# A three-layer network on one core: the delta rule's triangular inverses from blocks of 16 in place of 32, and a list scheduler that knows the array's tilings

## The chip, the cores and the metric

The kernel runs on one core of a Trainium2 chip. The core has a matrix engine (TensorE, PE in the profile, with its weight loads as PEld), VectorE (DVE), ScalarE (ACT), GpSimd (POOL) and a queue (SyncE, SP) from which DMAs are issued. The metric is device time in microseconds (us) per execution; lower is better.

## What is computed

A network of width 1024 on 512 tokens of x and 256 of context, batch 1. Block 1 has a gated delta rule mixer with 8 heads (GDN), a mixture of 16 experts on both regions, an SSD mixer with 8 groups, and a second mixture on x alone. Block 2 has an S5 and a short convolution mixer, a sparse attention (nsa), their projection (mix) and a feed-forward layer (ffn). The part that the change rewrites is the delta rule's solve. In the reference, per chunk and direction:

```python
kb = kc * bc[..., None]
lower = jnp.where(strict, jnp.einsum('nbhid,nbhjd->nbhij', kb, kc) * decay, 0.0)
rhs = jnp.concatenate([vc * bc[..., None], kb * jnp.exp(gcum)[..., None]], axis=-1)
sol = lax.linalg.triangular_solve(eye + lower, rhs, left_side=True, lower=True, unit_diagonal=True)
u, w = sol[..., :dv], sol[..., dv:]
attn = jnp.where(tril, jnp.einsum('nbhid,nbhjd->nbhij', qc, kc) * decay, 0.0)
def step(S, inp):
    q_i, k_i, u_i, w_i, a_i, g_i = inp
    v_new = u_i - jnp.einsum('bhck,bhkv->bhcv', w_i, S)
    o = (jnp.einsum('bhck,bhkv->bhcv', q_i * jnp.exp(g_i)[..., None], S)
         + jnp.einsum('bhij,bhjv->bhiv', a_i, v_new))
```

The kernel uses chunks of 128 tokens (6 of them: 4 of x, 2 of context) and inverts the unit triangular matrix of each chunk and direction explicitly.

## The kernel before, in words

**Recording and order.** All of a stage's code runs against a recorder (class Rec, line 53). Each instruction becomes an operation with the operations that it depends on and a cost in ns (cost, line 190); matmuls written under nc.together() are one operation. flush (line 243) turns the list into an order: schedule (line 307) is a list scheduler with simulated engines, which picks among up to 48 candidates per engine the one of highest priority that can start early enough. The priority is the place in the program less beta times the length of the work behind the operation, and an operation of lower priority goes first only if it can start more than tol ns sooner. flush takes the shortest of the (beta, tol) pairs that its caller gives, and emits the instructions in that order at line 304. So every instruction has line 304 in the profile, and each engine works through its own queue strictly in the emitted order. Costs in the model before: a matmul by its columns and passes, at one matmul at a time; a DMA lands 2.025 us after its issue at the earliest (1125 and 900 ns), and counts 2000 ns in the priorities. The callers' pairs: one for the GDN (line 946), one to four elsewhere.

**The GDN (line 577).** Each head projects q, k, v and z (px: matmuls with 512 and 256 columns over the two regions), forms G (k with k) and Hq (k with q), and from them L, the strictly triangular matrices of both directions in the two halves of one tile, and at. The inverse has two levels:

- Blocks of 32 on the diagonal. There are 4 x 6 x 2 = 48 per head. They go through DRAM (gdn_blocks, bscr in the code) into D32, one block per partition. DVE scales and masks them (two operations of 48 x 1024), and GpSimd inverts them row by row: 30 steps of two tensor_tensor each (x, then D). A memset sets the diagonal, ScalarE makes the transposed copy, one DMA takes both to DRAM (gdn_inverses, tscr in the code), and four DMAs bring them back as Td and Ud with chunks side by side. Eight ScalarE copies put Ud into U, whose off-diagonal blocks are zero.
- Joins to 64 and 128 on PE, for m = 32 and 64. pB multiplies L with the inverses at hand, ScalarE copies it to B, pU multiplies with the transposed inverses Tr, and ScalarE copies the negative into U. For m = 32 the transposed inverses are Td, for m = 64 PE makes them (pT).

The scan then runs 6 steps in each of the two directions: act_k with the state S, rt and U, vd with kT (the new state), vn with at, act_q with S. Behind it the outputs o are normalised on ACT and DVE, transposed on PE (oT), and go to DRAM. After all heads the out projection (op) follows; its last 48 matmuls belong to head 7. Some heads also carry rounds of the modulation (ada).

**The other stages** are recorded and ordered in the same way. In the SSD (line 1447) px and pcx are the projections, wl the low part of a weight tile that DVE makes for them, W the decay weights of a head: a DMA brings rows from DRAM (ssd_rows), ACT and DVE apply them, and py multiplies them with the inputs. In the mixtures eg, eu, ec and ey are the experts' matmuls, their weights come in pieces of 1 MB (we), and hT, pb, po, xs and others are transposes, gates, gather and scatter.

Of the kernel before, what the change touches and what calls it, by code (L numbers as in the profile page):

```python
# [52 lines left out]
class Rec:  # L53
# [4 lines left out]
    def __init__(self, nc, tc):  # L58
# [7 lines left out]
        self.slot_times = {}  # L66
        self.seen = set()
# [77 lines left out]
    def record(self, i, engine, method, a, k):  # L145
# [34 lines left out]
        cost = self.cost(engine, method, reads, writes, a, k)  # L180
        if i < len(self.ops):
# [4 lines left out]
            o["more"].append((method, a, k))  # L186
            return
        self.ops.append(dict(e=engine, m=method, a=a, k=k, preds=preds, names=names, cost=cost, psum=any(self.tiles.get(r[0], (0, 0, 0))[2] for r in rr + ww)))

    def cost(self, engine, method, reads, writes, a, k):  # L190
# [29 lines left out]
        if engine == "scalar":  # L220
            return (45.0 if psum else 95.0) + n / 1.2 + 93.0 * scalars + (90.0 if k.get("accum_out") is not None else 0)
# [21 lines left out]
    def flush(self, trials=((0.0, 30.0),)):  # L243
# [40 lines left out]
        cost = [2000.0 + o["cost"] / 360.0 if "dma" in o["m"] else o["cost"] for o in ops]  # L284
# [13 lines left out]
        self.span, self.seq, self.free_at, self.dma_free, times = best  # L298
# [8 lines left out]
    def schedule(self, static, beta, tol):  # L307
# [13 lines left out]
        for t, lst in order.items():  # L321
            for nm in lst:
                if nm in self.seen:
                    got.add(nm)
                    slots[t].remove(max(slots[t]))
                    alloc[t].add(pos[nm])
                    nxt[t] = pos[nm] + 1
        npred = [len(o["preds"]) for o in ops]
# [17 lines left out]
        while len(seq) < n:  # L346
            best = None
            for e, c in cand.items():
                fe = free_at[e]
                eb = None  # L350
                for r in c[: self.WINDOW]:
                    i = by[r]
                    st = max(fe, ready[i])
                    if eb is not None and st >= eb[0] - tol:
# [15 lines left out]
            if best is None:  # L370
                return math.inf, seq, free_at, dma_free, slots
# [15 lines left out]
            if "dma" in o["m"]:  # L387
                free_at[e] = st + 475.0
                dma_free = max(st + 1125.0, dma_free) + o["cost"] / 360.0
                fin = dma_free + 900.0  # L390
            else:
                fin = st + o["cost"]
                free_at[e] = fin
            end[i] = fin
# [12 lines left out]
        return max(end), seq, free_at, dma_free, slots  # L407
# [169 lines left out]
def gdn(K, H, apply, w, ba_w, conv_w, a_log, dt_b, norm_g, scr, bscr, tscr, rscr, side, xc, w_out, gate, route):  # L577
# [9 lines left out]
    es = ExitStack()  # L587
    K.ring(es, 15)
# [8 lines left out]
    low = per.tile([48, 32, 32], BF, name="low")  # L597
    for i in range(0, 32, 16):
        x = K.nm.tile([48, 16, 32], F32, name="low_f", tag="nm", bufs=3)
        m = K.cst[i:i + 16, 3, 0:32]  # L600
        nc.sync.dma_start(x, bass.AP(tensor=m.tensor, offset=m.offset, ap=[[0, 48]] + [list(z) for z in m.ap]))
        v.tensor_copy(low[:, i:i + 16, :], x)
# [86 lines left out]
    for h in range(NH):  # L689
# [75 lines left out]
        L = live.tile([128, 6, 128], F32, name="L", bufs=2)  # L765
        at = live.tile([128, 2, 6, 128], F32, name="at", bufs=2)
        for t0, t1 in ((0, 4), (4, 6)):
# [21 lines left out]
            for z in range(-1, 3):  # L789
                bl, cl, d = (slice(0, 128), slice(0, 128), 0) if z < 0 else (slice(32 * z, 32 * z + 32), slice(32 * z + 32, 128), 1)  # L790
                v.tensor_tensor(L[bl, t0:t1, cl], pT[bl, 0:n, cl], c_brk[d][bl, t0:t1, None].to_broadcast([bl.stop - bl.start, n, cl.stop - cl.start]), op=OP.mult)

# [3 lines left out]
        D32 = tmp.tile([48, 2080], F32, name="D32")  # L796
        nc.sync.dma_start(D32[:, 0:1056], bscr[h])
        T = D32[:, 0:1024].rearrange("p (i j) -> p i j", j=32)
        v.tensor_tensor(T, T, D32[:, None, 1024:1056].to_broadcast([48, 32, 32]), op=OP.mult)
# [6 lines left out]
        g_.memset(D32[:, 0:1024:33], 1.0)  # L806
# [1714 lines left out]
```

## Time and profile before

| | us |
|---|---|
| median of 3 timed runs | 3677.41 |
| the three runs | 3683.21, 3677.41, 3665.22 |
| the profiled execution | 3660.83 |
| its span | 3659.1 |

| engine | busy us | share of the span |
|---|---|---|
| PE | 3359.7 | 92% |
| PEld | 2255.5 | 62% |
| DVE | 1848.2 | 51% |
| ACT | 1181.0 | 32% |
| POOL | 555.4 | 15% |

The mean granted TensorE clock is 0.971 of the full 2.4 GHz. Since all instructions have one line, groups are told apart by tiles: px<-H,wl is the operation that writes px from H and wl. The stages by time: GDN to 774 us (its last sums and the routing to 870), first mixture to 1480, SSD to about 2014 and its out projection to 2160, second mixture to 2715, block 2 from there, with the attention in 2817 to 3013 and the feed-forward layer from 3289 to the end.

### The profile page before, as it was taken

To read this page: it belongs to the slowest core of one execution; us is meant where nothing else is said; L and a number is where in the kernel's file an instruction comes from. 1 tells how busy PE (TensorE), PEld (TensorE's weight loads), DVE (VectorE), ACT (ScalarE), POOL (GpSimd) and SP (SyncE) were. 2 spreads that over 40 slices of the span, in tenths; PEclk is the share of its full clock that TensorE was granted. 3 is DMA by queue.
4 is the path that set the end of the run, shared out by engine and by line. 5 is a ranking of instruction groups with operands and counts; after the bars stand their busy time and mean duration, and the time that the engine had idled before them with its cause. 6 is when DMAs were issued, how large, how long until landed. Compare 5 with 4: busy or idle time off the path is not lost. (4 is left out here: it accounts for less than half of the span.)

```text
span 3659.1 us, 55424 instructions
## 1 busy us (share of the span) xinstructions
PE 3359.7 (92%) x21505; PEld 2255.5 (62%) x21505; DVE 1848.2 (51%) x4086; ACT 1181.0 (32%) x2518; POOL 555.4 (15%) x753
## 2 busy tenths in 40 slices
PE   7987979899999999899999879888879999999999
PEld 4776765666344444677877654332257658878887
DVE  4666755562223222778778542452164564445542
ACT  3354543423111111355555321120032353333331
POOL 0646544301000000013222010010011000000000
PEclk9999989899999999999999889999999999999999
DMA  5522227455888888354241359999962303333322
GB/s 188 160 60 56 74 65 230 155 188 197 342 312 311 335 317 315 111 147 133 93 141 53 140 220 401 362 368 421 420 143 81 119 1 98 96 100 92 96 87 87
DMA packets 251652, 669.21 MB, mean 183 GB/s; under 512 B 72156, under 2 KB 85612, under 8 KB 202236
## 3 DMA queue, kind: packets, MB, share of 16 engines
q1 hardware_dynamic: 251388, 665.66, 51.4%
q8 instruction: 169, 2.77, 0.3%
q14 instruction: 95, 0.78, 0.1%
HBM read 644.26 MB, written 21.30 MB: 182 GB/s over the span
## 5 line engine op out<-in xcount | busy, mean ns | idle before, releaser
L304 DVE TENSOR_TENSOR wl<-w,wh 128x512 fp32r<-128x512 f32 (+3 forms) x452 | 323.1, 717 | 458.8 <-PE fu L304 68.0
L304 ACT ACTIVATE wh<-w 128x512 fp32r<-128x512 f32 (+3 forms) x500 | 307.7, 622 | 675.2 <-PE fu L304 120.7
L304 PE MATMUL eg<-we,xs 128*32 128x512 f32 (+1 forms) x1536 | 371.5, 596 | 8.3 <-DMA we<-moe_w 7.2
L304 PE MATMUL eu<-we,xs 128*32 128x512 f32 (+1 forms) x1536 | 322.3, 595 | 7.4 <-DMA we<-moe_w 7.4
L304 PE MATMUL ey<-we,hTs 128*32 128x512 f32 (+1 forms) x1536 | 295.1, 601 | 17.2 <-ACT hTs L304 9.0
L304 PE MATMUL px<-H,wl 128*128 128x512 f32 (+1 forms) x768 | 269.3, 372 | 21.4 <-DVE wl L304 21.3
L304 PE MATMUL px<-H1l,wh 128*128 128x512 f32 (+1 forms) x768 | 267.3, 364 | 0.0
L304 PE MATMUL px<-H,wh 128*128 128x512 f32 (+1 forms) x768 | 266.1, 370 | 0.5 <-ACT wh L304 0.3
L304 PE MATMUL ec<-we,xs 128*32 128x512 f32 x1024 | 235.2, 594 | 0.0
L304 DVE TENSOR_TENSOR yl<-ey,yh 64x512 fp32r<-64x512 f32 x64 | 44.1, 689 | 337.8 <-ACT yh L304 337.3
L304 PEld LDWEIGHTS eg<-we,xs 128*32 128x32 f32 (+1 forms) x1536 | 96.3, 118 | 140.2 <-issue 103.9
L304 POOL TENSOR_TENSOR wl<-w,wh 128x512 fp32r<-128x512 f32 x48 | 64.6, 1346 | 761.7 <-DVE H1l L304 658.1
L304 DVE SCALAR_TENSOR_TENSOR eth<-eth,eg 128x512 f32<-128x512 f32 x32 | 22.0, 687 | 310.8 <-ACT eth L304 310.8
L304 PEld LDWEIGHTS eu<-we,xs 128*32 128x32 f32 (+1 forms) x1536 | 91.9, 119 | 141.1 <-issue 105.8
L304 PEld LDWEIGHTS ey<-we,hTs 128*32 128x32 f32 (+1 forms) x1536 | 97.3, 120 | 127.6 <-issue 61.8
L304 PEld LDWEIGHTS px<-H,wl 128*128 128x128 f32 x768 | 143.1, 192 | 43.8 <-DVE wl L304 26.2
L304 ACT ACTIVATE eth<-eg 128x512 f32<-128x512 f32 x32 | 19.1, 595 | 462.0 <-PE eg L304 404.7
L304 PEld LDWEIGHTS px<-H,wh 128*128 128x128 f32 x768 | 144.3, 192 | 25.0 <-issue 6.1
L304 PEld LDWEIGHTS px<-H1l,wh 128*128 128x128 f32 x768 | 142.9, 192 | 18.6 <-issue 1.3
L304 PE MATMUL eyc<-we,hcTs 128*32 128x256 f32 x1024 | 140.9, 379 | 0.0
L304 POOL TENSOR_TENSOR D<-D,x 48x30 f32<-48x30 f32 (+14 forms) x240 | 133.7, 557 | 18.3
L304 POOL TENSOR_TENSOR x<-D 48x30 f32<-48x30 f32 (+14 forms) x240 | 127.0, 529 | 59.4 <-DVE D L304 41.5
(1040 smaller groups left out, 7564.1 us busy)
## 6 DMA issues: line engine op xcount, KB each, us to landing
we<-moe_w SPq DMA_DIRECT2D x384, 1024.0 KB, 7.9
w<-ada_w SPq DMA_DIRECT2D x192, 256.0 KB, 5.2
w<-w_gu SPq DMA_DIRECT2D x88, 256.0 KB, 3.4
w<-gdn_w SPq DMA_DIRECT2D x64, 256.0 KB, 3.1
w<-ssd_w SPq DMA_DIRECT2D x64, 256.0 KB, 3.1
w<-w_mix SPq DMA_DIRECT2D x48, 256.0 KB, 2.7
w<-w_dn SPq DMA_DIRECT2D x40, 256.0 KB, 2.6
w<-ssd_wz SPq DMA_DIRECT2D x32, 256.0 KB, 2.6
```

What stands on the lines that cost most here:

```text
L304: getattr(getattr(self.nc, o["e"]), m)(*a, **k)
```

## The change

Two parts. **The inverse.** The diagonal blocks have 16 rows and there are 96 of them, one per partition, in Dz, which also holds the transposed copies. GpSimd's chain has 14 steps instead of 30. They go out in two DMAs and come back as Td and Ud in the old form, with pairs of 16-blocks on the diagonal of 32-blocks. The join from 16 to 32 is new: qB multiplies L (for one direction) and Lb (for the other, a new tile of DVE) with Ud, DVE masks it with half into B16, qU multiplies with Td, and DVE writes Ud less qU into U (four operations, in place of ScalarE's eight copies). The join m = 32 now makes its transposes with pT, as m = 64 did.

**The order.** array gives each matmul a tiling of the array (its rows and columns rounded to 32, 64 or 128), a place in it and a time. schedule lets matmuls at different places overlap, and a change of tiling waits for the array to drain and 94 ns more. DVE operations that touch SBUF alone wait while GpSimd works. A DMA lands 500 ns later and counts 2500 ns, some strided ScalarE reads cost twice, and PE's times are divided by a clock of the stage (0.94 GDN, 0.99 mixtures, 0.96 SSD). Every flush tries 15 pairs of beta and tol and keeps the shortest. Instructions outside the GDN are the same in another order.

```diff
@@ class Rec @@
+    SWITCH = 94.0
...
+    def port(self, engine, method, reads, writes):
...
+        return engine == "gpsimd" or engine == "vector" and not any(self.tiles.get(x.tensor.name, (0, 0, 0))[2] for x in reads + writes)
...
+    def array(method, a):
...
+        size = lambda x: 32 if x <= 32 else 64 if x <= 64 else 128
+        lhs, n = a[1], free(a[2])
+        rows, cols = size(lhs.ap[0][1]), size(free(lhs))
+        r0, c0 = (x.offset // x.ap[0][0] % 128 if x.ap[0][0] else 0 for x in (lhs, a[0]))
...
+        d = (2 if two else 1) * n / 2.4 + (13.5 if lhs.dtype == F32R else 4.0)
...
+        return (rows, cols), (r0 // rows, c0 // cols), (2 if two else 1) * d
@@ cost @@
+            n *= 2 if any(x.ap[-1][0] > 16 and n > 512 for x in reads if x.ap[-1][1] > 1) else 1
@@ flush @@
-    def flush(self, trials=((0.0, 30.0),)):
+    TRIALS = tuple((b, t) for b in (0.0, 0.2, 0.4, 0.6, 1.0) for t in (0.0, 30.0, 90.0))
...
+    def flush(self, trials=TRIALS):
...
-        cost = [2000.0 + o["cost"] / 360.0 if "dma" in o["m"] else o["cost"] for o in ops]
+        cost = [2500.0 + o["cost"] / 360.0 if "dma" in o["m"] else o["cost"] for o in ops]
@@ schedule @@
+                    if e == "tensor":
+                        tiling, place, _ = ops[i]["pe"][0]
+                        st = max(st, held.get(place, 0.0) if tiling == mode else drained + self.SWITCH)
+                    elif e == "vector" and ops[i]["port"]:
+                        st = max(st, port)
...
-                fin = dma_free + 900.0
+                fin = dma_free + 1400.0
+            elif e == "tensor":
+                fin = at = st
+                for tiling, place, t in o["pe"]:
+                    t /= clock
+                    if tiling != mode:
+                        if mode is not None:
+                            at = max(at, drained + self.SWITCH)
+                        mode, held = tiling, {}
...
@@ gdn @@
-        for j in range(1, 31):
-            sh = [48, 31 - j, j]
-            x = tmp.tile([48, 240], F32, name="x32", bufs=2)[:, 0:sh[1] * sh[2]].rearrange("p (i j) -> p i j", j=j)
-            g_.tensor_tensor(x, T[:, j + 1:32, j:j + 1].to_broadcast(sh), T[:, j:j + 1, 0:j].to_broadcast(sh), op=OP.mult)
-            g_.tensor_tensor(T[:, j + 1:32, 0:j], T[:, j + 1:32, 0:j], x, op=OP.add)
+        for j in range(1, 15):
+            sh = [96, 15 - j, j]
+            x = tmp.tile([96, 64], F32, name="x16", bufs=2)[:, 0:sh[1] * sh[2]].rearrange("p (i j) -> p i j", j=j)
+            g_.tensor_tensor(x, T[:, j + 1:16, j:j + 1].to_broadcast(sh), T[:, j:j + 1, 0:j].to_broadcast(sh), op=OP.mult)
+            g_.tensor_tensor(T[:, j + 1:16, 0:j], T[:, j + 1:16, 0:j], x, op=OP.add)
...
-        for z in range(4):
-            bl = slice(32 * z, 32 * z + 32)
-            for d in range(2):
-                s.activation(U[bl, d, :, bl], Ud[bl, 1 - d], AF.Copy)
+        p = K.ps([128, 2, 6, 32], "qB")
+        with nc.together():
...
+                        pe.matmul(p[bl, d, t, :], Lb[bl, t, :] if d else L[bl, t, bl], Ud[bl, d, t, :], start=True, stop=True, skip_group_check=True)
+        B = tmp.tile([128, 2, 6, 32], F32, name="B16")
+        v.tensor_tensor(B, p, half[:, :, None, :].to_broadcast([128, 2, 6, 32]), op=OP.mult)
+        p = K.ps([128, 2, 6, 32], "qU")
+        with nc.together():
...
+                        pe.matmul(p[bl, d, t, :], Td[bl, d, t, :], B[bl, d, t, :], start=True, stop=True, skip_group_check=True)
+        for bl in rows:
+            v.scalar_tensor_tensor(U[bl, :, :, bl], p[bl], -1.0, Ud[bl], op0=OP.mult, op1=OP.add)
...
-    nc.flush(GDN_TRIALS)
+    nc.flush()
...
-GDN_TRIALS = ((0.4, 0.0),)
```

**The order, place 1: PE, the join of a head.** x24 is a group of 24 matmuls; p with a number is a matmul of the scan. Before, head 1 (an odd head):

```order
L304 MATMUL pB<-Ud,L 32x32 x24
L304 MATMUL row<-cst,cols 6x128
L304 MATMUL G<-act_k 128x128 x3
L304 MATMUL pU<-B_753,Td 32x32 x24
L304 MATMUL G<-act_k 128x128 x3
L304 MATMUL Hq<-act_q,act_k 128x128 x3
L304 MATMUL pT<-cst,U_337 64x64 x12
L304 MATMUL pB<-U_337,L 64x64 x12
L304 MATMUL GT<-cst,GE 128x128 x6
L304 MATMUL Hq<-act_q,act_k 128x128
L304 MATMUL pU<-B_758,Tr 64x64 x12
L304 MATMUL px<-H_313,wl 128x512
```

Head 2 (an even head) has only its own pB, pU, pB, pT, pU in one run, and then the scan. After, head 1:

```order
L340 MATMUL px<-H_319,wl 128x256
L340 MATMUL qU<-B_729,Td 32x32 x48
L340 MATMUL row<-cst,cols 6x128
L340 MATMUL pT<-cst,U_337 32x32 x24
L340 MATMUL pB<-U_337,L 32x32 x24
L340 MATMUL pU<-B_734,Tr_732 32x32 x24
L340 MATMUL pB<-U_337,L 64x64 x12
L340 MATMUL pT<-cst,U_337 64x64 x12
L340 MATMUL pU<-B_739,Tr_737 64x64 x12
L340 MATMUL p_743<-vb,U_337 128x128
L340 MATMUL p_750<-vb,U_337 128x128
L340 MATMUL p_748<-vn,at 128x128
```

The next head's G and Hq, which stood between the steps of the join, now stand ahead of qU; the px matmuls that stood within the scan stand behind it and ahead of qB. The same run of join and scan is found in heads 0 to 4, with four ada matmuls in head 4's join. The scan's matmuls stand in pairs, one of each direction.

**Place 2: PE, the end of the GDN, where head 7's outputs are transposed (oT).** Before:

```order
L304 MATMUL op<-H1l,wh 128x512
L304 MATMUL oT<-cst,o 128x128 x2
L304 MATMUL op<-G_2397,wl 128x512
L304 MATMUL oT<-cst,o 128x128 x3
L304 MATMUL op<-G_2398,wh 128x512
L304 MATMUL oT<-cst,o 128x128
L304 MATMUL op<-H1l,wh 128x512
```

After:

```order
L340 MATMUL p_2212<-rt,U_337 128x128
L340 MATMUL p_2219<-rt,U_337 128x128
L340 MATMUL p_2214<-vn,at 128x128
L340 MATMUL p_2221<-vn,at 128x128
L340 MATMUL oT<-cst,o 128x128 x6
L340 MATMUL op<-H1l,wh 128x512 x4
```

Before, oT stood among the out projection's matmuls with 158 of them behind it; after, it stands right behind head 7's scan with the last 48 behind it. The others moved ahead of the scan, into head 7's join.

**Place 3: DVE in the SSD, one head.** fm and y are the head's activations. Before, where these five rows come in each of four heads, and in a fifth with one wl:

```order
L304 SCALAR_TENSOR_TENSOR y<-y,sz_15111 128x512
L304 SCALAR_TENSOR_TENSOR fm_15182<-pcx,cw,fm_15182 128x255
L304 SCALAR_TENSOR_TENSOR W<-R,cs,W 128x128 x2
L304 TENSOR_TENSOR wl<-w,wh 128x512 x2
L304 SCALAR_TENSOR_TENSOR fm_15182<-th,fm_15182 128x768
```

After:

```order
L340 SCALAR_TENSOR_TENSOR fm_16233<-th,fm_16233 128x768
L340 SCALAR_TENSOR_TENSOR W<-R,cs,W 128x128 x8
L340 SCALAR_TENSOR_TENSOR y<-y,sz_16154 128x512
L340 TENSOR_TENSOR wl<-w,wh 128x512
L340 SCALAR_TENSOR_TENSOR y<-y,sz_16162 128x512
```

Two operations on W stood right ahead of wl; now eight stand together, with an operation on y between them and wl, and other heads have other neighbours.

## Rows read from the trace of the kernel before

**Rows 1.** Table of windows: window, its length, busy us of each engine, PEclk, DMA share, GB/s.
```profile
47.00:774.00 727.00, 638.95 (x4962) 506.09 (x4964) 450.34 (x1216) 317.78 (x761) 329.68 (x559) 0.94 0.38 115
...
870.00:1480.00 610.00, 599.95 (x5435) 267.39 (x5427) 163.08 (x345) 85.65 (x173) 0.29 (x2) 1.00 0.82 319
...
1520.00:2014.00 494.00, 464.61 (x2649) 390.51 (x2647) 394.73 (x788) 264.29 (x581) 129.19 (x90) 0.98 0.35 110
...
2160.00:2715.00 555.00, 485.43 (x2398) 203.04 (x2397) 205.02 (x457) 101.75 (x185) 40.14 (x29) 0.98 0.93 362
...
2817.00:3013.00 196.00, 184.36 (x891) 115.73 (x891) 124.37 (x391) 84.97 (x236) 0.00 (x0) 0.97 0.17 57
```

**Rows 2.** PE's waits in 47:774: in total, times, longest.
```profile
PE pB L304 <- DMA Ud<-gdn_inverses: 13.0, 5, 9.9
PE pB L304 <- DVE D L304: 12.9, 1, 12.9
PE pU L304 <- ACT B L304: 8.8, 5, 3.3
...
PE pB L304 <- POOL D L304: 2.7, 1, 2.7
PE pB L304 <- ACT U L304: 2.2, 2, 1.1
```

**Rows 3.** Timeline: start, length. GpSimd's last steps (head 0); head 4's way to pB.
```profile
173.61 0.23 POOL L304 TENSOR_TENSOR x<-D 48x30 f32<-48x30 f32 x1
173.92 0.24 POOL L304 TENSOR_TENSOR D<-D,x 48x30 f32<-48x30 f32 x1
...
474.24 0.15 POOL L304 MEMSET D<- 48x32 f32 x1
...
483.92 1.22 DVE L304 TENSOR_TENSOR D<-D 48x1024 f32<-48x1024 f32 x1 [5.19 <-DMA D<-gdn_blocks]
...
485.19 0.86 PE L304 MATMUL pB<-Ud,L 32*32 32x32 f32 x48 [12.85 <-DVE D L304]
```

**Rows 4.** Timeline of PE, early in the GDN.
```profile
53.70 0.40 PE L304 MATMUL baT<-H,wl 128*32 128x512 f32 x1
53.94 0.39 PE L304 MATMUL px<-H1l,wh 128*128 128x512 f32 x1
54.16 0.40 PE L304 MATMUL px<-H,wl 128*128 128x512 f32 x1
...
73.80 0.39 PE L304 MATMUL px<-H1l,wh 128*128 128x512 f32 x1
74.12 0.43 PE L304 MATMUL ba<-cst,ba__380 32*128 32x32 f32 x4
```

**Rows 5.** Timeline of PE, head 0's first join group at full clock.
```profile
186.94 0.61 PE L304 MATMUL pB<-Ud,L 32*32 32x32 f32 x48 [0.49 <-DMA Ud<-gdn_inverses]
```

**Rows 6.** Table of windows, the bare joins of heads 0 and 4.
```profile
187.00:199.50 12.50, 5.37 (x169) 4.72 (x169) 7.12 (x11) 9.02 (x23) 7.21 (x14) 0.73 0.20 57
...
485.20:499.00 13.80, 9.92 (x186) 9.04 (x186) 2.12 (x4) 8.02 (x24) 10.73 (x24) 0.50 0.01 1
```

**Rows 7.** Timeline of PE, head 0's scan.
```profile
205.44 0.39 PE L304 MATMUL p<-S,act_k 128*128 128x128 f32 x2
205.67 0.39 PE L304 MATMUL p<-S,act_q 128*128 128x128 f32 x2
...
208.75 0.49 PE L304 MATMUL p<-S,act_k 128*128 128x128 f32 x2
```

**Rows 8.** Timeline of PE, the first matmul behind head 6's scan.
```profile
677.36 2.00 PE L304 MATMUL oT<-cst,o 128*128 128x128 f32 x6 [9.99 <-DVE o L304]
```

**Rows 9.** The SSD: PE's wait for wl; DVE's timeline at one of them; W's DMAs.
```profile
PE px L304 <- DVE wl L304: 17.6, 9, 4.5
...
1845.97 0.64 DVE L304 SCALAR_TENSOR_TENSOR W<-R,cs,W 128x128 f32<-128x128 f32 x2 [2.23 <-ACT W L304]
1846.53 2.37 DVE L304 TENSOR_TENSOR wl<-w,wh 128x512 fp32r<-128x512 f32 x2
...
DMA to landing us min/median/max: 3.3/4.3/7.8
```

More of the change, by code (lines that the diff above doesn't have):

```diff
@@ L66, in __init__ @@
         self.slot_times = {}
+        self.array_at = None, {}, 0.0
+        self.clock = 1.0
         self.seen = set()
@@ L180, in record @@
         cost = self.cost(engine, method, reads, writes, a, k)
+        pe = self.array(method, a) if engine == "tensor" else None
         if i < len(self.ops):
@@ L297, in flush @@
         best = min((self.schedule(static, *x) for x in trials), key=lambda r: r[0])
[L298 removed]
+        self.span, self.seq, self.free_at, self.dma_free, times, self.array_at = best
         self.slot_times.update(times)
@@ L587, in gdn @@
     es = ExitStack()
+    nc.clock = 0.94
     K.ring(es, 15)
@@ L596, in gdn @@
         g_.memset(U, 0.0)
[L597 to L602, printed above, removed]
+    low = per.tile([96, 16, 16], F32, name="low")
+    m = K.cst[0:16, 3, 0:16]
+    nc.sync.dma_start(low, bass.AP(tensor=m.tensor, offset=m.offset, ap=[[0, 96]] + [list(z) for z in m.ap]))
+    Dz = per.tile([96, 2, 528], F32, name="Dz")
+    g_.memset(Dz, 0.0)
+    half = per.tile([128, 2, 32], F32, name="half")
+    v.memset(half, 0.0)
+    x = K.nm.tile([128, 2], F32, name="half_", tag="nm_s", bufs=3)
+    v.tensor_reduce(x[:, 0:1], K.ident.rearrange("p (z c) -> p z c", c=32)[:, :, 0:16], AX.XY, OP.add)
+    v.tensor_scalar(x[:, 1:2], x[:, 0:1], -1.0, 1.0, op0=OP.mult, op1=OP.add)
+    for d in range(2):
+        v.tensor_copy(half[:, d, 16 - 16 * d:32 - 16 * d], x[:, d:d + 1].to_broadcast([128, 16]))
     neg = K.nm.tile([24, 256], F32, name="neg", tag="nm", bufs=3)
@@ L806, in gdn @@
-        g_.memset(D32[:, 0:1024:33], 1.0)
-        s.activation(D32[:, 1056:2080].rearrange("p (i j) -> p i j", j=32), T.rearrange("p i j -> p j i"), AF.Copy)
+        D16 = tmp.tile([96, 528], F32, name="D16")
+        nc.sync.dma_start(D16[0:48, 0:512], bscr[h][:, 0:512])
+        nc.sync.dma_start(D16[0:48, 512:528], bscr[h][:, 1024:1040])
+        nc.sync.dma_start(D16[48:96, :], bscr[h][:, 528:1056])
+        T, Tt = (Dz[:, j, 0:512].rearrange("p (i j) -> p i j", j=32)[:, :, 0:16] for j in range(2))
@@ L810, in gdn @@
         Td, Ud = (tmp.tile([128, 2, 6, 32], F32, name=f"{n}d") for n in "TU")
-        for y, o0, step in ((Td, 0, 73728), (Ud, 24576, 24576)):
+        for y, o0, step in ((Td, 0, 73728), (Ud, 49152, -24576)):
             for d in range(2):
@@ L835, in gdn @@
                     for d, ra, ca in cut:
-                        pe.matmul(p[ra, t, :], L[ca, t, ra], Ud[ca, 1 - d, t, :] if m == 32 else U[ca, d, t, ca], start=True, stop=True, skip_group_check=True)
+                        pe.matmul(p[ra, t, :], L[ca, t, ra], U[ca, d, t, ca], start=True, stop=True, skip_group_check=True)
             B = tmp.tile([128, 6, m], F32, name=f"B{m}")
@@ L1144, in moe @@
     es0 = ExitStack()
+    nc.clock = 0.99
     pool = nc.pool(es0, "moe")
@@ L1296, in moe @@
                 gates(*P0[k - 1])
-    nc.flush(((0.0, 0.0),) if two else ((0.6, 30.0),))
+    nc.flush()
     es.close()
@@ L1456, in ssd @@
     es = ExitStack()
+    nc.clock = 0.96
     K.ring(es, 18)
```

84 lines of the change are left out of this document (58 added, 26 removed).

## The prediction

> **What bounds the kernel now.** The first view to read is the table of windows, which cuts the span into stages. TensorE (PE) is busy for 638.95 of the 727 us of the gated delta rule, 599.95 of 610 in the first mixture of experts, 464.61 of 494 in the SSD mixer and 184.36 of 196 in the window with block 2's attention [rows 1]. These stages end when PE's work ends, so a microsecond of PE work or PE idleness is a microsecond of time. The second mixture differs: its DMA share is 0.93 [rows 1], so what PE saves there I count at nothing.
>
> The second view is the list of waits. In the delta rule it names what the change aims at: the joining matmul pB waited 13.0 us for Ud, the inverse on its way back from DRAM, and 12.9 us in one place that is put down to DVE's D [rows 2]. That one is head 4, and the timeline shows that the D on DVE (483.92) is the next head's, which had itself waited for a load: GpSimd's last step on head 4's blocks is the memset at 474.24, and pB starts at 485.19, 12.85 us after PE ran dry [rows 3]. So 25.9 us are waits for the chain GpSimd, ScalarE copy, DMA out, DMA in. The other pB and pU waits (8.8, 2.7 and 2.2 us [rows 2]) lie inside the join, between its own short steps: 13.7 us.
>
> The third view is the order of both programs, shown above. Before, odd heads have other matmuls between the join's steps and even heads have none. After, heads 0 to 4 have next to none, neither in the join nor in the scan behind it.
>
> **The change part by part: the delta rule.** (a) GpSimd does 28 short operations per head in place of 60. Its short ones start 0.31 us apart (173.61, 173.92 [rows 3]), so the chain is about 28 x 0.31 = 8.7 us. PE's order puts some 142 px matmuls between one head's scan and the next head's qB, half of them with 512 columns at 0.22 us (53.94 to 54.16 [rows 4]) and half with 256, which I take at half of that: 23 us. GpSimd's first step stands at the end of the scan; from there 8.7 us plus the 10.95 us that memset to pB took [rows 3] are 19.7. The waits should go, with 3 us to spare: **-25.9 us**.
>
> (b) New PE work per head: qB 48 matmuls, qU 48, pT 24, all 32x32. A group of 24 (48 records) took 0.61 us at full clock [rows 5]; five such groups are 3.05 us, times 8 heads **+24.4 us**. The nearest slow row is the same group at the half clock, 0.86 us [rows 3], so the upper end is +34. The row gives 13 ns a record; the four blocks of a chunk stand at four places of the array. The Trainium skill, TensorEngine Tiling (Array Packing), section Performance Considerations (Instruction Overhead), says that a matmul has some 60 cycles of overhead and that no tiling factor should be taken from a dimension that is already small; 60 cycles at 2.4 GHz are 25 ns, and by that 240 records would cost 6.0 us a head, 48 us in all. The row speaks against that here, and it is a rival below.
>
> (c) The join. It is now qU, four DVE subtractions into U, pT and pB, a ScalarE copy, pU, four ScalarE copies, and the 64 level as before. Head 4's bare join ran from 485.2 to 499 with PE busy 9.92 of 13.8 us, so 3.9 idle; head 0's from 187 to 199.5 with 5.37 of 12.5, so 7.1 idle [rows 6]. The four DVE operations have 384 columns where two of 128 took 0.64 us [rows 9]: between 4 x 0.32 = 1.3 and 4 x 0.96 = 3.8 us; I take 2.2. A bare join then idles 6.1 to 9.3 us; I take 6, near head 4's, because head 0's was stretched by other work in ScalarE's queue. Five heads make 30 (up to 46), in place of 13.7: **+16 us** (0 to +33).
>
> (d) The scan. In a bare scan one direction comes round in 3.31 us (act_k at 205.44 and 208.75), while one operation costs 0.23 (205.44 to 205.67 [rows 7]) and ten of them 2.3; 1.0 is lost per step, about 5 per head. Before, three heads were bare; after, six (0 to 4, and 7). The new order takes both directions in pairs, which may lose less or nothing more, so 0 to +16: **+7 us**.
>
> (e) The end. oT waited 9.99 us for DVE's o behind head 6's scan [rows 8], where PE had nothing else. Head 7 had op matmuls there; after, all that can go first have gone, and oT stands right behind the scan. I price it by head 6's: **+10 us** (0 to +14).
>
> (f) The clock. Behind head 4's wait the join ran at 0.50, the 1.2 GHz level, throughout; behind head 0's short waits at 0.73 on average [rows 6]. At half clock, half of the busy time is lost: 5.0 us in head 4's window, about 1.7 in head 0's. Heads 2 and 4 gain 3.3 each, heads 1 and 3 newly lose 1.7 each: **-3 us**.
>
> **Changes of tiling, all stages.** A 512-column matmul is followed after 0.22 us by one of the same tiling, and after 0.32 us where the next uses another (73.80 to 74.12). But baT, with 32 columns, gave way to px after 0.24 (53.70 to 53.94): those are nearly free [rows 4]. So a change costs about 0.1 us, less what is free; I use 0.092 and count, over both programs, only changes in which baT and the SSD's dtT (a lone narrow matmul too) have no part. They go from 126 to 100 in the delta rule, 201 to 132 in the first mixture, 39 to 26 in the SSD, 111 to 35 in block 2's first part. That is -2.4, **-6.3**, -1.2 and **-7.0 us**. The second mixture's 38 would be -3.5, counted at 0.
>
> **The SSD.** px waited 17.6 us for wl in nine places. In the timeline of one, DVE's W<-R waited 2.23 us for ScalarE's W, and wl stood behind it [rows 9]. W's rows come by DMA with 3.3 to 7.8 us to landing [rows 9], where the old schedule reckoned with about 2 us and the new one with 2.5. In the new order wl no longer follows a pair of W<-R in each head. I take 14 of the 17.6: **-14 us** (0 to -17.6). A doubled cost of one kind of ScalarE read and GpSimd's hold on DVE only move places in the order; I count them within this.
>
> **The sum.** Delta rule: -25.9 + 24.4 + 16 + 7 + 10 - 3 - 2.4 = +26. Elsewhere: -6.3 - 1.2 - 14 - 7.0 = -28.5. Together -2.5 us against the profiled execution's 3660.83. The three timed runs have the median 3677.41, 16.6 above it; on that footing the forecast is **3675 us**: no change, by the bound of 0.5% (18 us) that such a measurement can resolve.
>
> **The rivals.** *The new order hides what I count as bare.* If paired scans lose nothing more, the joins stay at 13.7 us and the end is covered, the delta rule comes to -25.9 + 24.4 - 6.6 (the clock of heads 2 and 4 wholly regained is 3.3 x 2) - 2.4 = -10; with the SSD's whole 17.6 and 1.2, 13.3 of tilings and the mixture's 3.5 the sum is -46: **3631 us**. For it: the waits of the join are short steps that could be ordered better; against it: the order shows no filler. 0.35.
>
> *The bare joins pull the clock down* (slower). PE's join is a few short groups with pauses; head 4's stayed at the 1.2 GHz level for all of it [rows 6]. If all five bare joins go that way, each loses 5.0 rather than 1.7 us, +16, and idles the upper 9.3, +17: 3675 + 33 = **3708 us**. It decides once a join's PE idle exceeds about 8 us or its window shows 0.50. The Trainium skill, TensorE: Matmul & The Clock Gate, Part 1, says that the low clock is the default and activity releases it; the trace agrees with 0.50 behind a 12.85 us wait. For it: head 0's 0.73 without a long wait. 0.18.
>
> *The DMAs and not GpSimd set the inverse's arrival.* Memset to pB was 10.95 us; the new form has two stores in that chain where one was. If it takes 8 us longer, the 3 us to spare are gone and qB waits 5 us in six heads: **3705 us**. Against: less to copy and to store at a time. 0.07.
>
> *Small matmuls go out one by one at 25 ns.* +24 us: **3699 us**. Against: 13 ns per record [rows 5]. 0.02.
>
> **How the numbers follow.** The forecast has 0.38, the faster rival 0.35, the slower ones 0.27 together. The range goes from 3620 to 3730: below, beyond the faster rival's 3631 by a few microseconds of unseen gains in ordering; above, to the slower clock (3708) with qB's and the matmuls' upper end (+10) and part of the SSD's 14 not gained. Chances: faster by over 0.5% 0.35, within 0.38, slower 0.27.
>
> **What would show it.** Right: no pB or qB wait for Ud over 2 us; bursts of qB and qU at 1.2 us; GpSimd busy some 100 us instead of 329.68 in the delta rule; px waiting for wl under 5 us in the SSD; the first mixture 6 us shorter. Wrong: a join whose steps leave PE idle under 4 us or over 8, a scan step at 2.4 us or below, an oT of head 7 that doesn't wait, half-clock stretches of over 10 us behind joins, or qB waiting for DMA.

## The result and the profile after

The changed kernel takes 3631.91 us in the median of four runs (3624.51 to 3634.77), the kernel before 3673.55 in four runs beside it (3665.22 to 3683.21): a ratio of **0.9883, 95% interval 0.9852 to 0.9914**. That is faster by 1.2%, beyond the 0.5% that such a measurement can resolve, and 43 us under the forecast. The profiled execution took 3634.77 us, with a span of 3633.0 against 3659.1 before. These two executions lie 26 us apart where the medians lie 42 apart: the one profiled before (3660.83) was faster than all four that were timed, and the one profiled after is the slowest of its four. The stages below account for the 26.

The table of windows of the changed kernel, cut at its own stage ends (columns as in [rows 1]); the second row is the stretch from the delta rule's last matmul to the first expert's:

```profile
46.60:779.60 733.00, 657.45 (x6871) 533.69 (x6869) 446.52 (x1323) 285.94 (x705) 127.54 (x302) 0.94 0.36 108
780.00:891.00 111.00, 81.80 (x744) 56.80 (x741) 49.24 (x111) 39.00 (x101) 15.94 (x17) 0.84 0.38 135
891.00:1477.00 586.00, 578.35 (x5452) 211.99 (x5451) 164.00 (x351) 83.56 (x171) 0.46 (x2) 0.99 0.85 334
1515.00:2010.00 495.00, 467.33 (x2678) 393.27 (x2678) 390.26 (x801) 266.24 (x588) 123.32 (x89) 0.98 0.35 110
2152.60:2648.00 495.40, 442.33 (x2156) 175.06 (x2158) 163.57 (x375) 80.47 (x148) 40.66 (x30) 0.98 0.95 386
```

A stage's windows are wider or narrower here than those of [rows 1], so the stages were also cut in both traces at the same instructions (first px, last op, first eg, and so on). That gives, in us of the profiled executions:

| stage | before | after | moved | forecast |
|---|---|---|---|---|
| delta rule | 725.5 | 733.0 | +7.5 | +26 |
| from there to the first expert (called the passage below) | 96.6 | 111.5 | +14.9 | 0 |
| first mixture, with what follows it up to the SSD | 641.4 | 624.0 | -17.4 | -6.3 |
| SSD, with its output | 646.7 | 637.5 | -9.2 | -15.2 |
| second mixture | 503.9 | 495.5 | -8.4 | 0 |
| block 2's first part | 360.1 | 344.9 | -15.2 | -7.0 |
| block 2's rest | 637.3 | 640.0 | +2.7 | 0 |

The sum is -25.1; the first px starting 0.9 us earlier makes it the -26.1 of the spans. So the change wins outside the delta rule, by the order alone, and loses 22 us in the delta rule and behind it, where the new inverse is. Single executions scatter: in the runs below whose order of a stage is the changed kernel's but for some places, the delta rule took 733.0 to 739.9 us, the first mixture's row 617.6 to 624.0, the SSD's 633.7 to 640.7 and block 2's first part 341.1 to 345.3. A move of a few us in one row shows nothing by itself.

PE's waits in the delta rule of the changed kernel (total, times, longest), against [rows 2]:

```profile
PE oT L340 <- DVE o L340: 14.4, 2, 8.3
PE pT L340 <- DVE U L340: 13.5, 20, 2.0
PE p L340 <- ACT vd L340: 8.3, 26, 1.3
PE pB L340 <- ACT U L340: 6.0, 6, 1.1
...
PE qU L340 <- issue: 3.9, 3, 1.9
PE pU L340 <- ACT Tr L340: 3.5, 6, 0.6
...
PE pU L340 <- ACT B L340: 2.1, 5, 0.4
...
PE qB L340 <- DMA Ud<-gdn_inverses: 0.3, 1, 0.3
```

The waits for the inverse on its way are gone: qB waits 0.3 us once, where pB had 25.9 us in two kinds. In their place stand short steps of the join itself.

And the passage, by PE's waits there and by the issues on SP's queue:

```profile
PE ada L340 <- DMA w<-ada_w: 19.4, 3, 17.7
```

```profile
794.70 2.89 SPq L340 DMA_DIRECT2D we<-moe_w  x6
797.64 1.96 SPq L340 DMA_DIRECT2D w<-ada_w  x3
```

```profile
SPq L340 <- PE lgT L340: 19.3, 1, 19.3
SPq L340 <- ACT lg__2464 L340: 6.7, 1, 6.7
```

The first expert weights are issued at 794.70 (before: 760.72), because the queue waits 19.3 us for PE's lgT and 6.7 for ScalarE's lg ahead of them: lgT and lg are the last readers of the router's tile, so the place that the weights are loaded into must now overlap it. ada's weights stand behind them in the queue, and PE waits 17.7 us for those. What moved the addresses are the small tiles that the change adds to the delta rule's pools, as the fourth run below shows. Neither the prediction nor any wait of before spoke of this.

### The profile page after: what moved, and what is told of

The parts are those of the page before. It is cut to its first block, busy times and chain, and to the rows that moved or that the text cites. A ratio compares the mean times of both kernels' runs of the same rounds, so it can differ in the third digit from the quotient of the medians.

```text
span 3633.0 us, 59178 instructions
## 1 busy us (share of the span) xinstructions
PE 3327.6 (92%) x23425; PEld 2223.0 (61%) x23425; DVE 1829.5 (50%) x4193; ACT 1142.0 (31%) x2462; POOL 347.6 (10%) x498
## 5 line engine op out<-in xcount | busy, mean ns | idle before, releaser
L340 DVE TENSOR_TENSOR wl<-w,wh 128x512 fp32r<-128x512 f32 (+3 forms) x452 | 310.4, 691 | 370.9 <-PE dn L340 59.1
L340 PE MATMUL eg<-we,xs 128*32 128x512 f32 (+1 forms) x1536 | 288.7, 600 | 6.7 <-DMA we<-moe_w 6.7
L340 PE MATMUL px<-H,wl 128*128 128x512 f32 (+1 forms) x768 | 261.9, 367 | 10.6 <-DVE wl L340 9.7
L340 PE MATMUL eu<-we,xs 128*32 128x512 f32 (+1 forms) x1536 | 259.9, 598 | 7.1 <-DMA we<-moe_w 6.9
L340 PE MATMUL ey<-we,hTs 128*32 128x512 f32 (+1 forms) x1536 | 243.4, 600 | 12.8 <-ACT hTs L340 10.3
L340 PE MATMUL ec<-we,xs 128*32 128x512 f32 x1024 | 173.7, 592 | 0.1
L340 PEld LDWEIGHTS eg<-we,xs 128*32 128x32 f32 (+1 forms) x1536 | 75.5, 119 | 148.0 <-issue 124.5
L340 PEld LDWEIGHTS eu<-we,xs 128*32 128x32 f32 (+1 forms) x1536 | 71.5, 120 | 154.0 <-issue 129.1
L340 PEld LDWEIGHTS ey<-we,hTs 128*32 128x32 f32 (+1 forms) x1536 | 67.5, 120 | 141.2 <-issue 106.4
L340 PEld LDWEIGHTS px<-H1l,wh 128*128 128x128 f32 x768 | 137.4, 190 | 17.6
L340 ACT ACTIVATE yh<-ey 64x512 fp32r<-64x512 f32 x64 | 37.9, 592 | 274.2 <-PE ey L340 260.4
L340 DVE SCALAR_TENSOR_TENSOR X<-po,mod,X 128x512 f32<-128x512 f32 x128 | 87.8, 741 | 44.3 <-PE po L340 44.0
L340 PE MATMUL ada<-w,sc 128*32 128x512 f32 x384 | 83.5, 644 | 26.4 <-DMA w<-ada_w 26.0
```

The source lines that it names most:

```text
L340: getattr(getattr(self.nc, o["e"]), m)(*a, **k)
```

## The experiments

Twelve kernels, each timed beside the kernel before; ratios are to it. First the two halves of the change apart.

**The inverse alone**, in the recorder and with the pairs of before.

```diff
 recorder, pairs and all later stages: as before
-def gdn(...):  # blocks of 32
+def gdn(...):  # the change's, flushed with ((0.4, 0.0),)
```

> The new inverse with the recorder, the costs and the (beta, tol) pairs of before in every stage. In its order every join has 18 to 31 other matmuls between its steps and every scan 41 or more, while in the changed kernel heads 0 to 4 have none and 4. Theory A (the inverse is worth its 25.9 us of waits, but the changed kernel's order spends them on bare joins and bare scans): the delta rule, from the first px to the last op, takes 700 to 715 us, against 725.5 before and 733.0 with the change; in all 3645 to 3660 us, the later stages as before. Theory B (the 24 us of new matmuls eat the waits, whatever the order): the delta rule within 5 us of 725.5, in all 3668 to 3680 us.

Measured: 3681.63 us, 1.0038 (1.0023 to 1.0054). The delta rule shrank by 5.3 us (720.2), between what the two theories said, and the passage grew to 118.3 by the same wait for ada (18.1 us). The waits for the inverse are bought off with some 22 us of new matmuls; the passage takes more than what is left.

**The order alone**, with the inverse of before.

```diff
 recorder, clock and pairs of every stage: the change's
-def gdn(...):  # blocks of 16
+def gdn(...):  # blocks of 32, as before
```

> The old inverse with the new recorder and its 15 pairs everywhere. Joins and scans are as bare as in the changed kernel (heads 0 to 2 and 4). Theory A: the waits for the GpSimd chain come back beside the bare joins, the delta rule takes 745 us or more, in all 3640 us or more. Theory B: the delta rule is no longer than the changed kernel's 733 us, in all 3625 to 3635 us. Both theories: mixture, SSD and block 2 as in the changed kernel.

Measured: 3654.05 us, 0.9963 (0.9950 to 0.9977). The delta rule is 778.9 us, as theory A said. So the new inverse is worth 46 us under the change's recorder (778.9 to 733.0) and 5 under the old one. It is not its own wait alone that it saves: here PE waits 16.0 us for Ud, and 32.3 for DVE's act_k and act_v ahead of the transposes tr; in all it idles 121.0 us against 75.6.

**The delta rule as before, the rest as changed**: code, recorder's model and pair of before up to its flush.

```diff
+    nc.old = True     # the model of before, for this flush
     K.ring(es, 15)
...
+    nc.flush(((0.4, 0.0),)); nc.old = False
```

> The delta rule with the code, costs and pair of before, every later stage with the new recorder. If the gain is the later stages' alone, and the change's delta rule and the boundary behind it lose 6.6 and 14.8 us, this takes 3632 - 21 = 3611 us, and the stretch from the last op to the first eg has 97 us instead of 111.5. If the first mixture's 23.6 us are only what the late start of its weights left to catch up, this takes about 3630 us and the first mixture is near 610 us again.

Measured: 3599.43 us, 0.9816 (0.9798 to 0.9834): 32 us below the changed kernel, and 12 below the lower of the two expected times. The delta rule is 722.8 and the passage 91.8; the first mixture, to its last scatter matmul, is 5 us shorter than the changed kernel's, and every later stage within 3 us of it.

**The small tiles moved**, nothing else: Dz, half and Lb in the pool of temporaries, low padded.

```diff
-    Dz = per.tile([96, 2, 528], F32, name="Dz")
+    Dz = tmp.tile([96, 2, 528], F32, name="Dz")
-    half = per.tile(...);  Lb = live.tile(..., bufs=1)
+    half = tmp.tile(...);  Lb = tmp.tile(..., bufs=1)
```

> The changed kernel with Dz, half and Lb placed in another pool of SBUF (and low padded to its old bytes). With that the same 15 pairs lead to another order in the delta rule: 21 to 33 other matmuls in each join and 25 or more in each scan. Nothing else differs. Theory A: the delta rule takes 700 to 715 us instead of 733.0, in all 3605 to 3620 us. Theory B: within 8 us of the changed kernel's 3632 us, with the bubbles found elsewhere.

What this expectation says of filled joins was misread from another kernel's order; in the trace its joins are as bare as the changed kernel's. Measured: 3608.23 us, 0.9836 (0.9818 to 0.9854). The delta rule stays at 734.0 (theory B's), and the time still falls into theory A's range, by the passage: it goes from 111.5 to 91.7, as ada's wait is 1.7 us in place of 19.4. In all the runs this wait goes with the placing: 18.8 to 20.2 us in the first, fifth, sixth and eighth, which have the new tiles unmoved, and 0.5 to 1.7 in the eight others.

**Tilings free in the model**, everywhere.

```diff
-    st = max(st, held.get(place, 0.0) if tiling == mode else drained + self.SWITCH)
+    st = max(st, held.get((tiling, place), 0.0))
```

> The changed kernel whose model lets a change of tiling cost nothing and wait for nothing; places in the array, clock, port, DMA latencies and the 15 pairs stay. Its order in the delta rule has filled joins and scans (21 to 33 and 25 to 50 other matmuls per head) with the new inverse. Theory T (the tilings in the model make the later stages' gain): the first mixture to its last scatter matmul goes back from 602.3 to 620 to 630 us and block 2's first part from 344.9 to 352 to 360, while the delta rule falls to 715 to 722 us; in all 3645 to 3670 us. Theory P (the gain is from the pairs and the other numbers): mixture and block 2 within 5 us of the changed kernel, in all 3615 to 3625 us.

Measured: 3696.39 us, 1.0078 (1.0049 to 1.0106). The stages part, the way of theory T but not by its sizes: the delta rule is 678.8 (-54 against the changed kernel) and the SSD's first stretch 481.1 (-14), but the passage is 162.8, the first mixture to its last scatter 612.3 (+10), the second 520.0 and block 2's first part 397.9 (+53). In the latter the changes of tiling are 328 against 35, and PE's waits are alike (37.3 and 36.5 us), so each change costs 53 / 293 = 0.18 us. PE's timeline there shows it, first this run, then the changed kernel:

```profile
2740.17 0.49 PE L340 MATMUL cv<-H2l,wh 128*128 128x512 f32 x1
2740.60 0.43 PE L340 MATMUL y<-cwi,Sb 128*64 128x128 f32 x2
2740.96 0.49 PE L340 MATMUL cv<-H2h,wl 128*128 128x512 f32 x1
2741.38 0.43 PE L340 MATMUL y<-cwi,Sb 128*64 128x128 f32 x2
```

```profile
2740.11 0.39 PE L340 MATMUL cv<-H2l,wh 128*128 128x512 f32 x1
2740.34 0.39 PE L340 MATMUL cv<-H2h,wl 128*128 128x512 f32 x1
2740.56 0.39 PE L340 MATMUL cv<-H2h,wh 128*128 128x512 f32 x1
```

A cv is followed by its like after 0.23 us, by a y of another tiling after 0.42 to 0.43. In the passage of this run the clock adds to it: behind the wait for ada (18 us, the placing is the changed kernel's) it stands at 0.66 and 0.61, and xs costs 490 ns a piece where the third run has 335.

```profile
800.00:840.00 40.00, 40.00 (x182) 24.55 (x180) 6.26 (x12) 14.11 (x39) 7.27 (x7) 0.66 0.00 0
840.00:888.00 48.00, 47.31 (x285) 30.70 (x284) 5.88 (x16) 13.18 (x30) 4.97 (x6) 0.61 0.06 20
```

**GpSimd's hold on DVE out of the model.**

```diff
-                if e == "gpsimd":
-                    port = fin
```

> The changed kernel whose model doesn't let GpSimd hold up DVE. Theory T: no stage moves by more than 5 us but for the boundary behind the delta rule, where the first weights of the experts still wait for the routing; in all 3625 to 3640 us. Rival (the port in the model is what shortened the SSD, 502.4 to 495.2 us): the SSD is back at 500 us or more, in all 3638 us or more.

Measured: 3628.14 us, 0.9887 (0.9854 to 0.9920), the changed kernel's time. The SSD's first stretch is 504.0 in place of 495.2, as the rival said, but the time isn't longer; in total the term does nothing that can be measured.

**The new inverse ordered by the old model**, tiles moved, later stages as changed.

```diff
+    nc.old = True
...
-    nc.flush()
+    nc.flush(((0.4, 0.0),)); nc.old = False
```

> The delta rule with the new inverse, but ordered by the costs and the pair of before (joins with 22 to 31 other matmuls, scans with 41 to 67), its new tiles placed so that the experts' first weights don't wait for the routing; later stages with the new recorder. Beside the run with the delta rule as before (3599 us), only the inverse differs. Theory A (in a filled order the inverse still is worth its waits): the delta rule 700 to 710 us, in all 3577 to 3590 us. Theory B (the new matmuls eat the waits): the delta rule 718 to 724 us, the boundary 92 to 97, in all 3593 to 3603 us.

Measured: 3596.89 us, 0.9806 (0.9776 to 0.9836). The delta rule is 722.0 with the new inverse, 722.8 with the old one under the same model and pair (third run), as theory B said. The old kernel's 725.5 and the third run's 722.8 have one order between them, so neither these 0.8 us nor the 5 of the first run are clear of the scatter: by the old model, which puts other work into the wait, the new inverse is worth nothing that can be measured.

**The callers' pairs of before**, with the new model.

```diff
-    nc.flush()      # 15 pairs, the best by the model
+    nc.flush(...)   # outside the delta rule: each caller's own, as before
```

> The changed kernel, but behind the delta rule each stage tries only the pairs of beta and tol that its caller gave before, by the new costs. Theory T: the costs make the order, the later stages stay within 5 us of the changed kernel's, in all 3625 to 3640 us. Theory P: the first mixture and block 2's first part lose over half of their 27 and 15 us, in all 3650 us or more.

Measured: 3672.63 us, 1.0004 (0.9985 to 1.0023). The whole gain is gone, though not in every stage: the SSD's first stretch is 28 us longer (523.3, and 21 longer than before the change), the second mixture 11 (506.4); the first mixture and what follows it are 624.1 against 624.0, block 2's first part 348.4 against 344.9. Theory P's time came, but not its stages. (The delta rule, ordered alike, came out at 739.9, 7 us longer and at a mean clock of 0.93 against 0.94; why is not shown.) So under the new costs the SSD and the second mixture need the choice among 15 pairs, and block 2's first part does not. The first mixture is mixed: to its last scatter it is 612.5 here, 602.3 in the changed kernel and 629.4 before. What 15 pairs would do with the old costs, no run shows.

**Tilings free in the delta rule alone**, tiles moved.

```diff
+    nc.tilings = False      # at the delta rule's start: the edit of the fifth run, by a flag
...
     nc.flush()
+    nc.tilings = True
```

> The changed kernel with two edits: while the delta rule's stretch is ordered, a change of tiling costs nothing in the model (as in the run without tilings, but there alone; all later stretches keep the tilings), and the new small tiles lie in the pool of temporaries, so that the experts' first weights don't land on the router's tile. Theory T (the 94 ns that the model asks for a change of tiling keeps other work out of the joins and scans, and that alone made the changed kernel's delta rule 733 us): the delta rule's stretch 670 to 690 us, as in the run without tilings, the stretch to the first expert 90 to 98 as in the run with moved tiles, the first mixture 597 to 603, the rest as in the changed kernel: time 3555 to 3570. Theory R (what the delta rule's stretch gains is work pushed behind it, as the 162.8 us after it in the run without tilings would say): 679 and then 130 to 165, time 3600 to 3640.

Measured: 3563.61 us, 0.9716 (0.9689 to 0.9742). Theory T: the delta rule is 684.0, the passage 94.4, the first mixture to its last scatter 598.8. Against the run with moved tiles alone, the edit takes 50 us off the delta rule and 45 off the time, so little comes back. It makes *more* changes of tiling there, 175 against 97. The edit takes two things out of the model at once, the 94 ns and the wait until the array has drained; which of them keeps the other work out is not shown. What it buys is seen in head 0's join, first PE's timeline of the changed kernel, then of this run (each from qB on):

```profile
183.67 0.58 PE L340 MATMUL qB<-Ud,Lb 32*32 32x32 f32 x46
184.17 0.27 PE L340 MATMUL row<-cst,cols 128*6 128x128 f32 x1
185.90 0.92 PE L340 MATMUL qU<-B,Td 32*32 32x32 f32 x82 [1.45 <-issue]
187.31 0.43 PE L340 MATMUL qU<-B,Td 32*32 32x32 f32 x14 [0.50 <-issue]
188.49 0.28 PE L340 MATMUL pT<-cst,U 32*32 32x32 f32 x2 [0.75 <-DVE U L340]
...
191.94 0.87 PE L340 MATMUL pU<-B,Tr 32*32 32x32 f32 x48 [0.42 <-ACT B L340]
193.92 1.23 PE L340 MATMUL pB<-U,L 64*64 64x64 f32 x18 [1.11 <-ACT U L340]
```

```profile
203.30 0.58 PE L341 MATMUL qB<-Ud,Lb 32*32 32x32 f32 x46
203.81 0.61 PE L341 MATMUL px<-H,wl 128*128 128x256 f32 x2
204.26 0.51 PE L341 MATMUL px<-H,wh 128*128 128x512 f32 x2
204.61 0.51 PE L341 MATMUL px<-H1l,wh 128*128 128x256 f32 x2
205.05 0.99 PE L341 MATMUL qU<-B,Td 32*32 32x32 f32 x93
206.66 0.25 PE L341 MATMUL qU<-B,Td 32*32 32x32 f32 x3 [0.62 <-issue]
206.84 0.33 PE L341 MATMUL oT<-cst,o 128*128 128x128 f32 x1
...
210.69 0.69 PE L341 MATMUL pT<-cst,U 32*32 32x32 f32 x46
```

And the windows of the two joins, again the changed kernel's first:

```profile
183.20:199.10 15.90, 9.71 (x409) 8.25 (x409) 8.43 (x20) 5.36 (x15) 0.00 (x0) 0.61 0.10 23
```

```profile
202.80:216.00 13.20, 12.58 (x424) 10.65 (x425) 9.83 (x30) 5.31 (x12) 0.00 (x0) 1.00 0.09 34
```

The bare join idles 6.2 us and runs at 0.61, the filled one idles 0.6 and keeps 1.00. The scans behind it are filled as well: 33 to 62 other matmuls in each here, 4 or fewer in heads 0 to 4 of the changed kernel. Over the whole delta rule PE's idle time falls from 75.6 to 35.1 us (73.9 in the run with moved tiles alone), the time at the half clock from 92 to 15.

**The same in the SSD's first stretch too.**

```diff
+    nc.tilings = False      # at the SSD's start, True again behind its first flush
```

> As the run before, and a change of tiling is also free in the model while the state space stage's first stretch is ordered. Theory T: that stage's first stretch 478 to 485 us as in the run without tilings (changed kernel 495.2), time 12 to 16 below the run before, 3541 to 3557. Rival (the 14 us there came from the stage starting elsewhere, behind another mixture): 492 to 497, and the time of the run before.

Measured: **3545.55 us, 0.9663 (0.9641 to 0.9684)**, 18 below the run before, a little more than theory T said: the SSD's first stretch is 482.9 (495.6 in the run before), its output 141.2 (-1.0), the second mixture 495.7 (+0.3). This version is the fastest of all; it beats the changed kernel by 86 us.

**The old inverse in that version.**

```diff
-def gdn(...):  # blocks of 16
+def gdn(...):  # blocks of 32, as before; flushed with tilings free
```

> As the run before, with the inverse of before (blocks of 32, scanned on GpSimd) in the delta rule. Theory A (with the joins filled, the new inverse is worth what it takes off GpSimd's chain, since PE then reaches pB early): the delta rule's stretch 700 to 730 us, 20 to 50 above the run before. Theory B (the new inverse is worth nothing once PE has other work for the wait, as between the two runs that order it by the model of before, 722.0 against 722.8): within 6 us of the run before.

Measured: 3610.82 us, 0.9842 (0.9821 to 0.9862), the delta rule 743.5. The inverse is worth 60 us here, theory A's side and more than its 50; but not where A put it. PE's waits up to 725 us, in a delta rule from 48 to 792:

```profile
PE oT L341 <- DVE o L341: 28.1, 16, 12.3
PE tr L341 <- DVE act_k L341: 24.3, 4, 6.4
PE tr L341 <- DVE act_v L341: 12.4, 7, 5.9
PE pB L341 <- DMA Ud<-gdn_inverses: 8.9, 4, 6.0
```

Only 8.9 us are for the inverse itself. PE runs dry ahead of the next head's transposes: in this order the px stand ahead of oT (in one head the last px starts at 310.15, the last oT at 314.24 and tr, with nothing between, at 320.47). The order is not the run before's with another inverse in it, but planned anew. So what the inverse is worth is a property of the pair, inverse and order: 46 and 60 us in two plannings, and nothing measurable in the old one.

**Tilings priced, tolerance 200 ns**, delta rule alone, tiles moved.

```diff
-    nc.flush()
+    nc.flush(tuple((b, 200.0) for b in (0.0, 0.2, 0.4, 0.6, 1.0)))
```

> The changed kernel with the small tiles moved (as in the run of moved tiles alone, delta rule 734.0) and the tilings kept in the model of the delta rule, 94 ns included; only the pairs of that stretch are others: the tolerance, within which a more urgent operation goes ahead of one that could start sooner, is 200 ns in all of them, where the list of the changed kernel ends at 90. PE's order then has some 15 other matmuls in every join and 6 to 16 in every scan. Theory G (not the 94 ns itself but the rule that the operation that can start first goes first makes the joins bare: 94 lies above every tolerance tried, so px always runs out before the join): the delta rule's stretch 690 to 710, time 3565 to 3585. Theory P (a price on tilings is wrong here, however the choice is made): 720 to 740, time 3595 to 3615.

Measured: 3612.21 us, 0.9831 (0.9810 to 0.9853), the delta rule 735.0. Theory G falls: the joins are filled (from a head's first pT to its last pU stand 10 to 18 others, and it takes 6.4 to 8.2 us; in heads 0 to 3 of the changed kernel none, and 9.6 to 10.1) and yet nothing is won. The scans stayed thin, 6 to 20 others, and their matmuls with their waits take 127.8 us where the ninth run has 105.0; and PE waits elsewhere (total, times, longest):

```profile
PE qU L340 <- issue: 9.7, 6, 4.5
PE tr L340 <- DVE act_v L340: 6.6, 4, 3.9
...
PE tr L340 <- DVE act_k L340: 4.1, 1, 4.1
```

PE idles 52.7 us, and 55 us stand at the half clock against 15 in the ninth run. Eight of its ten stretches begin within 3.5 us of the start of a PE wait of 2.0 to 4.5 us (for tr from 125.4 and 148.4, for qU from 221.2 and 594.2, and so on; the clock falls at 127.8, 151.7, 223.4 and 595.4). That theory P's number came out does not show P's reason: whether a tiling price with a better choice of pairs would win here stays open.

## Why the prediction was right or wrong

The range (3620 to 3730) held the time; the likeliest case, no change, did not come. The time came out at the faster rival's 3631, though not by that rival's sum: it put the delta rule at -10 and the joins at 13.7 us, and the delta rule was +7.5 with bare joins. That the range held is in part luck. On the profiled executions the sum was -2.5 and the spans moved by -26.1: the delta rule came out 18.5 us below its forecast, the passage 14.9 above and the later stages together 19 below. Another 19.5 of the 43 us come from the step to the median: the profiled execution of before lay 16.6 us below it, the one after 2.9 above. By its own steps:

**(a) The waits for the inverse, -25.9: right.** qB's one wait is 0.3 us. The last GpSimd step of head 0 is over at 173.71, qB runs at 183.23. GpSimd is busy 127.5 us in the delta rule, a little above the 100 or so that was named.

**(b) The new matmuls, +24.4: right.** From the first qB of head 1 to the next other matmul it is 0.95 us for its 96 records, 9.9 ns each, or 19.8 for each of the 48 matmuls, which have two records apiece; qB, qU and the 32 level's pT come to 23.3 in all, their waits left out. The Trainium skill, TensorEngine Tiling (Array Packing), section Performance Considerations (Instruction Overhead), would have put 60 cycles on each matmul, by estimate 25 ns at 2.4 GHz; the trace does not agree, for 32x32 blocks that lie at four places of the array.

```profile
243.98 0.59 PE L340 MATMUL qB<-Ud,L 32*32 32x32 f32 x46
...
244.42 0.58 PE L340 MATMUL qB<-Ud,Lb 32*32 32x32 f32 x46
244.93 0.85 PE L340 MATMUL ssq<-sq,ones 128*32 128x384 f32 x8
```

**(c) The bare joins, +16: right.** Head 0's idles 6.2 us where 6 were taken; the joins' waits are 29.9 us in all, in place of 15.5 before besides the inverse's, +14.4.

**(d), (e) and the rest of the delta rule: the sum failed here, by 18.5 us.** Summed from the start of each matmul to the start of the next, by the product that it makes, and with each wait counted to the matmul that waited, the delta rule's time went so (us, the waits in it in brackets; the version of the ninth run beside it):

| product | before | after | ninth run |
|---|---|---|---|
| p, the scan | 120.0 (4.5) | 141.5 (14.4) | 105.0 (2.9) |
| qB, qU, pT, pB, pU | 74.9 (41.4) | 90.8 (29.9) | 54.6 (7.3) |
| px | 298.0 (4.2) | 281.7 (2.4) | 310.4 (6.3) |
| oT, op | 100.3 (18.5) | 100.5 (19.4) | 79.4 (3.6) |
| ada, adat | 59.0 (4.6) | 58.6 (6.5) | 67.7 (7.5) |
| all others | 73.2 (13.4) | 59.9 (2.5) | 66.8 (5.1) |

The joins moved by +15.9, about the +14.5 that (a), (b) and (c) make together. The scan lost 21.5 where (d) took 7 out of a range of 0 to 16, but px, which had no term and in the new order runs in one piece instead of in the scans' gaps, takes 16.3 less. The two belong together: scan and px went from 418.0 to 423.2, and these 5.2 are near (d)'s 7. Two steps failed. One is (e), priced at +10: head 7's oT did wait, 6.1 us, and head 6's 8.3 in place of 9.99 [rows 8], but the four smaller waits of oT, 6.3 us, went, and oT and op together moved by 0.2. The other is a term that the sum did not have: all other products take 13.3 us less, 10.9 of it in waits, of tr (5.4 us before, 1.8 after), of row (4.5 before) and of ssqT (2.0). The new order did this and not the inverse, for the first run has the new inverse in the old order and waits 11.7 us for tr and 4.5 for row; which part of the model did it is not shown.

**(f) The clock, -3: wrong in sign, small.** The half clock holds 92 us in the delta rule against 86, about +3 (it lies within the rows of the table). The slower rival's mechanism was there (0.61 in head 0's join against the 0.73 of [rows 6]), and the delta rule pays for it: the ninth run shows what its absence gives, together with that of the idle time.

**Changes of tiling, 0.092 us: the mis-sized term outside the delta rule.** Block 2's first part had 76 fewer changes and lost 15.2 us, 0.20 each; the second mixture 38 fewer and 8.4, 0.22; the fifth run gives 0.18 by the other way round. The row that gave 0.1 [rows 4] is one step, from px to the small ba; the step from cv to y in the fifth run costs 0.2. Of the 69 changes that the forecast gave to the first mixture, 16 lie in the passage; at 0.2 in place of 0.092 the other 53 are 10.6 of its 17.4 us. That the second mixture's gain was counted at nothing, as DMA was 0.93 of the time [rows 1], was wrong: 8.4 us came, at a DMA share of 0.95. But the eighth run has as few changes there (90 against 95) and no gain: there and in the SSD it hangs on the pairs, so a price per change is a reading of block 2 above all.

**The SSD, -14: half.** px waits 8.2 us for wl in place of the 17.6 of [rows 9], but other waits stand beside it (those of ptr are new, py waited 6.3 before), and the stage with its output won 9.2:

```profile
PE px L340 <- DVE wl L340: 8.2, 6, 3.4
PE py L340 <- DVE W L340: 7.2, 5, 4.5
PE ptr L340 <- DVE fm L340: 5.3, 3, 1.8
PE ptr L340 <- ACT wh L340: 3.3, 1, 3.3
```

**The passage, +14.9: not foreseen.** The forecast looked at what each transfer waits for within the delta rule and not at which tile's memory the next stage's first load reuses.

## What to carry to other kernels

A planner that knows a true cost can still order worse: a change of tiling does cost about 0.2 us here, and pricing it, with the wait for the array to drain, shortened block 2, but in the delta rule it kept other work out of short dependent chains. Without it the delta rule was 50 us shorter, 39 of them PE's idle time. Switch such a term stage by stage, and read what a faster link in a chain is worth only together with the order around it. Where a change adds tiles to a pool, look at what the next stage's first loads now wait for: 20 us of this change were an address.

## What the runs showed of the hardware

Two things were not expected. Going back and forth between two tilings cost 0.18 us a change in the fifth run, 0.20 by the change itself in block 2, about twice what a single step from a wide to a small matmul shows (0.1 [rows 4]). And the granted clock can fall behind short waits: in the last run, eight waits of 2.0 to 4.5 us were each followed by a stretch at the 1.2 GHz level, and its ten stretches last 5.5 us on average. Not every such wait does it: in the ninth run one of 2.1 us (px for wl, from 278.0) was followed by no fall. That run, with 78 more changes of tiling than the changed kernel but few waits, had 15 us of the low level in 684.
